# Second feed-forward block: narrower matmuls in its first quarter, and other engines for the weight split in its other three

## The chip, the core and the metric

The kernel runs on one core of a Trainium2 chip. The metric is the device time of one execution in microseconds (us). Two runs of the kernel before took 2849.98 and 2848.92 us, with a median of 2849.45 us.

The engines are named as the profile names them: PE is TensorE's matrix multiplication, PEld its weight loads, DVE is VectorE, ACT is ScalarE, POOL is GpSimd and SP is SyncE, which here issues DMAs. "Columns" of a matmul are the columns of its moving operand; the stationary operand (the "weights" of the array) is 128 x 128 in all matmuls of this text unless said otherwise.

## The reference

One layer of a diffusion trunk over 384 tokens (128 context, 256 latent) of width 2048: a half-step feed-forward block, a mixer (attention and gating), a second half-step feed-forward block, and a final norm.

```python
def swiglu_sublayer(x, g, w_gate, w_up, w_down, shift, scale, gate):
    h = rms_norm(x, g) * (1 + scale) + shift
    f = (jax.nn.silu(h @ w_gate) * (h @ w_up)) @ w_down
    return x + 0.5 * gate * f
...
x_ctx = swiglu_sublayer(x_ctx, ffn2_norm[l], ffn2_w_gate[l], ffn2_w_up[l], ffn2_w_down[l],
                        m_ctx[6], m_ctx[7], m_ctx[8])
...
y_prompt = rms_norm(x_ctx, final_norm)
```

The hidden width is 5632, that is 44 blocks of 128. All tensors are 32-bit floats.

## The kernel before, in words

**The product in three parts.** Activations and weights are each split into an upper part (rounded to the type fp32r) and a lower part (what is left, fp32r too). A product of 128 x 128 weights with one block of activations is three matmuls into the same PSUM bank (`three`): lower weights by upper activations (L256), upper by lower (L257), upper by upper (L258). Each moves 384 columns (386 in a phase's first group, where two extra columns carry the shift). In the built program each matmul has its own weight load; L257 and L258 load the same upper weights one after the other.

**The weight stream.** Weights lie in DRAM as chunks of 128 x 2048 numbers (1 MB). SP loads a chunk into one of three `raw` buffers (`pump`, L205). `ahead` splits one half chunk (128 x 1024) at a time: ACT casts it into a `whi` buffer (L221), then DVE subtracts that from the raw half into a `wlo` buffer (L225). There are four `whi` and four `wlo` buffers. `half`, called by `prod_w` ahead of the matmuls of every half chunk, calls `ahead`, which splits up to the half chunk three places further on; its buffers are those of the half chunk just before the present one. A half chunk feeds 24 matmuls: four banks, two row blocks, three parts.

**The second feed-forward block.** The hidden blocks are cut in quarters of 6, 6, 6 and 4 groups of two hidden blocks (`QUARTERS`). In a quarter each group (`group_gu`; the first of all is `first_group`) takes eight half chunks for its four products (two gate, two up), over all 16 row blocks of the input; `glu` makes silu(gate) * up of them and splits it into `gh` and `gl`. Then `down` multiplies the quarter's hidden blocks by the down weights: four output groups (`dg`) of four banks, each over six half chunks (four in the last quarter). The first three quarters' sums are kept in `x` (`put_y`); the last quarter's are added to x by `add_x`, two DVE instructions for each bank (L578).

**PSUM banks.** Three of a group's four banks come in turn from five `acc` buffers, the fourth from three `mp` buffers.

**Beside it.** Until half chunk 150 after the output projection, modulation tiles are handled: POOL issues a 0.5 MB DMA (`adaw`, L395), DVE multiplies and sums it (L410). That takes in the first two quarters of the second block. In the last quarter `join` reads x back from DRAM (`xo`) and adds it.

**Order.** The program is written out by hand: each engine carries out its instructions in the order of the code, and waits only for the buffers and data it needs.

Of the kernel before, what the change touches and what calls it, by code (L numbers as in the profile page):

```python
# [42 lines left out]
NSEL = 4  # L43
# Half chunks of the weight stream beside which other work is issued: the cached
# keys of each group, the pieces of x kept in DRAM, the splits ahead of the
# groups' ends (LATE), and the modulation tiles (SP0, SP; NREST of them go beside W_out).
KSL = (0, 0, 0, 6)
# [23 lines left out]
def stage_halves(st):  # L71
    """The (group, row block) pairs of each half chunk of a stage."""
    k0, k1 = BLOCKS[st]
    pairs = [(g, k) for g in range(G0) for k in range(k0, k1)]
    return [pairs[i:i + 2] for i in range(0, len(pairs), 2)]


def plan():
    """The order in which the weight chunks are consumed: 'A' chunks go to the
    modulation vectors as they are, 'W' chunks are split for the products."""  # L80
    kinds, pieces = [], []
# [33 lines left out]
class Kernel:  # L115
    def __init__(self, ctx, tc, a):
        self.ctx, self.tc, self.nc, self.a = ctx, tc, tc.nc, a

    # ---------------------------------------------------------------- pools
    def setup(self):  # L120
# [33 lines left out]
        self.late = True  # L154
        self.wide = False
        self.defer = deque()
        self.room = 0
# [6 lines left out]
    def later(self, slot, fn):  # L164
        """Runs fn beside the given half chunk of the stream."""
        self.at.setdefault(max(slot, self.slot), []).append(fn)
# [15 lines left out]

    # -------------------------------------------------------- weight stream
    def pump(self):
        """Loads the next chunks, in the order of use, as far as buffers are free."""
        nc = self.nc
# [22 lines left out]
    def ahead(self, n=NWP, between=None):  # L209
        """Splits the next half chunks, as far as buffers are free; between runs  # L210
        after the first upper part."""
        nc = self.nc
        while len(self.split) < n and self.next_split < len(self.pieces):
            c, half = self.pieces[self.next_split]
            if half is not None:
                if c not in self.raw:
                    break
                src = self.raw[c][:, half * 1024:(half + 1) * 1024]
                hi = self.wp.tile([P, 1024], F32R, tag="whi", name="whi")
                lo = self.wp.tile([P, 1024], F32R, tag="wlo", name="wlo")  # L220
                nc.scalar.copy(hi, src)  # L221
                if between is not None:
                    between()
                    between = None
                nc.vector.tensor_sub(lo, src, hi.bitcast(F32))  # L225
                self.split[self.next_split] = (hi, lo)
                if half == 1:
                    self.done(c)
            self.next_split += 1
# [6 lines left out]
    def half(self):  # L236
        """The next half chunk's two parts; runs what goes beside it."""
        if not self.late or self.pos not in self.split:
# [12 lines left out]

    # ------------------------------------------------------------- products
    def three(self, bank, wh, wl, xh, xl, first, last, n):
        nc = self.nc
        o, xh, xl = bank[:, :n], xh[:, :n], xl[:, :n]
        nc.tensor.matmul(o, lhsT=wl, rhs=xh, start=first, stop=False)  # L256
        nc.tensor.matmul(o, lhsT=wh, rhs=xl, start=False, stop=False)  # L257
        nc.tensor.matmul(o, lhsT=wh, rhs=xh, start=False, stop=last)  # L258

    def prod_w(self, banks, xs, kts, first, last, after=None, n=T):  # L260
        """banks[u] += W[kts, u]^T @ xs[kts] over one half chunk."""
        hi, lo = self.half()
# [8 lines left out]
    def prod_x(self, banks, xs, kts, first, last, after=None):  # L271
        """banks[tt] += xs[kts, tt]^T @ W[kts] over one half chunk."""
        nc = self.nc
# [15 lines left out]

    # ----------------------------------------------------------- modulation  # L290
    def ada_rows(self):
        """silu of both conditioning vectors, padded to 32 stationary columns."""
        nc = self.nc
# [37 lines left out]
    def ada_unit(self, sb, unit, nk):  # L331
        """The rows of sums become columns, added over the four column groups."""
        nc = self.nc
# [24 lines left out]
    def scales(self, j, cg, k0=0, k1=KT):  # L358
        """s = norm gain * (1 + scale) of modulation triple j."""
        nc = self.nc  # L360
# [7 lines left out]
    def csb_load(self, kh, slot):  # L368
        """silu of half of both conditioning vectors, on all partitions."""
        nc = self.nc  # L370
# [46 lines left out]

    # ----------------------------------------------------------------- norm
    def square(self, src):
# [11 lines left out]
    def grown(self, kt, ssq, raw, settle=True):  # L431
        """A new row block of x goes into the norm and, if it may, into the next
        operand; what the vector engine does of it comes one block later."""
        if raw:
# [15 lines left out]
    def rstd(self, sums, width):  # L450
        """1 / sqrt(mean + eps) of each token, on all partitions."""
        nc = self.nc
# [31 lines left out]
    def make_raw(self, *kts):  # L484
        """x scaled, without the token's norm factor and the shift."""
        for kt in kts:
# [24 lines left out]
    def raw_out(self, src, rs):  # L511
        """The products of the raw operand: the tokens' part times their norm
        factor, and the shift's part, to be added to it."""
        nc = self.nc
# [5 lines left out]

    # ------------------------------------------------------------------ ffn
    def glu(self, gi, u, src, rs=None, c=None):
# [25 lines left out]
    def lagged(self):  # L548
        """The lower part of the last g, which need not hold up what comes next."""
        if self.lag is not None:  # L550
# [3 lines left out]
    def first_group(self, ssq, after):  # L554
        """A phase's first group: on the raw operand, while the norm factors and
        the rest of the phase's operand are made. after(u, bank, rs) ends it."""
        banks = [self.bank(u) for u in range(4)]
# [23 lines left out]
    def put_y(self, kt, src, first):  # L581
        """The sum over the quarters' products, where x was."""
        if first:
# [4 lines left out]
    def join(self, ng, src, gate):  # L588
        """Beside the up products of the last quarter: x + gate * y."""
        free = range(2 * ng, 2 * G0)  # L590
# [58 lines left out]
    def first_quarter_staged(self):  # L649
        """The first groups over one block of rows at a time, with the partial  # L650
        sums kept where the groups' products will lie."""
        nc = self.nc
# [63 lines left out]

    # ---------------------------------------------------------------- mixer
    def open_mix(self, st):
# [55 lines left out]

    # attention of one head pair, in pieces
    def att_bias(self, pair, e):
# [103 lines left out]

    # gMLP
    def group_vg(self, j):
# [65 lines left out]
    def out_h(self, rs, *kts):  # L948
        """The mixer's own normalized outputs take h's place."""
        nc = self.nc  # L950
# [55 lines left out]
    def mixer_tail(self, hf):  # L1006
        """The gated half of the mixer's outputs, made beside the other half's products."""
        if hf == 0:
# [28 lines left out]

    # ----------------------------------------------------------------- all
    def spread(self, runs, first, end):
        """The queued modulation tiles, evenly over the half chunks first to end  # L1040
        that end no group; runs: how many of them, and for which half of the
        conditioning vectors (None: the one that is there)."""
        gap = ACTD + 2
# [12 lines left out]
    def run(self):  # L1056
# [90 lines left out]
        with ExitStack() as st:  # L1147
# [8 lines left out]
            for qi, n in enumerate(QUARTERS):  # L1156
                if qi == len(QUARTERS) - 1:
                    self.half_gate(8)
                    self.join(n, self.keep, self.m[8])
                for g in range(n):  # L1160
                    if qi == 0 and g == 0:
                        self.first_group(ssq, lambda u, bank, rs: self.glu(0, u, bank, rs))
                    else:
                        self.group_gu(g)
                lastq = qi == len(QUARTERS) - 1
                if lastq:
                    ssq = self.tmp("ssq")
# [11 lines left out]
def chunks(w, cols):  # L1179
    """[rows, n] -> [128, 2048] blocks of the columns given as slices, each of  # L1180
    as many 128-row parts side by side as fit."""
    import numpy as np
# [122 lines left out]
```

## Time and profile before

| | |
|---|---|
| runs | 2849.98 and 2848.92 us, median 2849.45 us |
| profiled execution | span 2848.6 us, the only time that the page gives of it; 0.85 us under the median of the runs |
| PE busy | 2816.9 us, 99% of the span |
| DVE busy | 1820.1 us, 64% |
| ACT busy | 1018.3 us, 36% |
| POOL busy | 155.5 us, 5% |
| granted TensorE clock | 0.997 |
| DMA | 524.91 MB, mean 184 GB/s |

A row of the groups of instructions reads: line, engine, operation, tile written <- tiles read, shape, count | busy us, mean ns of one | idle time of the engine just before them and what ended it. Matmuls are pipelined, so that the duration in a matmul's row is longer than the distance from one start to the next; that distance is read from the timeline or from a window's length and count. A row of the windows view gives the stretch, the busy time (and count) of PE, PEld, DVE, ACT and POOL, the granted clock, the DMA engines' share and the GB/s.

### The profile page before, as it was taken

To read this page: it belongs to the slowest core of one execution; us is meant where nothing else is said; L and a number is where in the kernel's file an instruction comes from. 1 tells how busy PE (TensorE), PEld (TensorE's weight loads), DVE (VectorE), ACT (ScalarE), POOL (GpSimd) and SP (SyncE) were. 2 spreads that over 40 slices of the span, in tenths; PEclk is the share of its full clock that TensorE was granted. 3 is DMA by queue.
4 is the path that set the end of the run, shared out by engine and by line. 5 is a ranking of instruction groups with operands and counts; after the bars stand their busy time and mean duration, and the time that the engine had idled before them with its cause. 6 is when DMAs were issued, how large, how long until landed. Compare 5 with 4: busy or idle time off the path is not lost.

```text
span 2848.6 us, 39204 instructions
## 1 busy us (share of the span) xinstructions
PE 2816.9 (99%) x16054; PEld 2719.1 (95%) x16054; DVE 1820.1 (64%) x2851; ACT 1018.3 (36%) x1453; POOL 155.5 (5%) x270
## 2 busy tenths in 40 slices
PE   7999999999999999999999999999999999999997
PEld 6889999999999999988888999999999999999997
DVE  4777888789888788764555888444444543333345
ACT  3345433322332234553334535333333223322342
POOL 0000011011111010000000000000000000000000
PEclk9999999999999999999999999999999999999999
DMA  8874566666666675444332663444444433333432
GB/s 335 306 283 173 191 236 231 223 228 247 233 226 240 232 255 200 157 160 145 115 119 104 245 234 128 163 163 148 174 145 164 154 139 120 128 124 127 167 126 85
DMA packets 98308, 524.91 MB, mean 184 GB/s; under 512 B 10832, under 2 KB 18384, under 8 KB 52176
## 3 DMA queue, kind: packets, MB, share of 16 engines
q1 hardware_dynamic: 61648, 371.39, 36.1%
q0 software_dynamic: 36480, 151.01, 15.2%
q8 instruction: 126, 2.06, 0.3%
q14 instruction: 54, 0.44, 0.0%
HBM read 511.88 MB, written 10.49 MB: 183 GB/s over the span
## 4 chain that ended last, share of the span: by engine, by line
PE 52%; DVE 0%; ACT 0%; issue 0%; DVEq 0%
PE acc L256 13%; PE acc L258 12%; PE acc L257 12%; PE mp L256 4%; PE mp L258 4%; PE mp L257 4%; PE acc L281 1%; PE acc L282 1%; PE acc L283 1%; PE mp L796 1%; DVE x L1173 0%; PE mp L870 0%; PE mp L840 0%; PE mp L916 0%; PE mp L456 0%; PE mp L865 0%
## 5 line engine op out<-in xcount | busy, mean ns | idle before, releaser
L225 DVE TENSOR_TENSOR wlo<-raw,whi 128x1024 fp32r<-128x1024 f32 x640 | 783.5, 1226 | 841.1 <-ACT whi L221 840.2
L221 ACT CAST whi<-raw 128x1024 fp32r<-128x1024 f32 x640 | 670.7, 1049 | 1421.4 <-PE mp L258 1148.7
L256 PE MATMUL acc<-hh,wlo 128*128 128x384 f32 (+1 forms) x2760 | 939.7, 340 | 0.0
L258 PE MATMUL acc<-hh,whi 128*128 128x384 f32 (+1 forms) x2760 | 933.0, 338 | 0.0
L257 PE MATMUL acc<-hl,whi 128*128 128x384 f32 (+1 forms) x2760 | 931.0, 337 | 0.0
L256 PEld LDWEIGHTS acc<-hh,wlo 128*128 128x128 f32 x2760 | 519.7, 188 | 31.8 <-issue 16.5
L257 PEld LDWEIGHTS acc<-hl,whi 128*128 128x128 f32 x2760 | 521.0, 189 | 0.8
L258 PEld LDWEIGHTS acc<-hh,whi 128*128 128x128 f32 x2760 | 519.7, 188 | 0.0
L256 PE MATMUL acc<-gh,wlo 128*128 128x384 f32 x1056 | 357.7, 339 | 0.4 <-ACT x L584 0.4
L257 PE MATMUL acc<-gl,whi 128*128 128x384 f32 x1056 | 354.3, 336 | 0.0
L258 PE MATMUL acc<-gh,whi 128*128 128x384 f32 x1056 | 352.8, 334 | 0.0
L410 DVE CUSTOM_DVE_ANT_0 scr<-adaw,csb,m 128x1024 bf16<-128x1024 f32 x208 | 266.8, 1283 | 3.8
L410 DVE CUSTOM_DVE_ANT_0 scr<-adaw,csb,par 128x1024 bf16<-128x1024 f32 x208 | 266.7, 1282 | 3.7
L258 PE MATMUL mp<-hh,whi 128*128 128x384 f32 (+1 forms) x688 | 232.4, 338 | 0.0
L256 PE MATMUL mp<-hh,wlo 128*128 128x384 f32 (+1 forms) x688 | 231.8, 337 | 0.0
L257 PE MATMUL mp<-hl,whi 128*128 128x384 f32 (+1 forms) x688 | 231.6, 337 | 0.0
L256 PEld LDWEIGHTS acc<-gh,wlo 128*128 128x128 f32 x1056 | 198.0, 188 | 0.7 <-ACT x L584 0.7
L258 PEld LDWEIGHTS acc<-gh,whi 128*128 128x128 f32 x1056 | 198.5, 188 | 0.0
L257 PEld LDWEIGHTS acc<-gl,whi 128*128 128x128 f32 x1056 | 198.3, 188 | 0.0
L395 POOL DMA_DIRECT2D adaw<-wada_t x208 | 110.1, 530 | 1457.2 <-DVE m L410 1378.8
L257 PEld LDWEIGHTS mp<-hl,whi 128*128 128x128 f32 x688 | 129.7, 189 | 0.0
L256 PEld LDWEIGHTS mp<-hh,wlo 128*128 128x128 f32 x688 | 129.5, 188 | 0.0
(163 smaller groups left out, 2251.0 us busy)
## 6 DMA issues: line engine op xcount, KB each, us to landing
raw<-ws SPq DMA_DIRECT2D x320, 1024.0 KB, 4.9
adaw<-wada_t POOLq DMA_DIRECT2D x208, 512.0 KB, 4.1
rawa<-wada_s POOLq DMA_DIRECT2D x34, 1024.0 KB, 5.7
csb<-crow POOLq DMA_DIRECT2D x6, 1024.0 KB, 7.6
keep<-x SPq DMA_DIRECT2D x8, 768.0 KB, 7.4
rawa<-wada_s SPq DMA_DIRECT2D x5, 1024.0 KB, 6.6
bias<-bias SPq DMA_DIRECT2D x16, 256.0 KB, 5.1
xo<-xT SPq DMA_DIRECT2D x16, 192.0 KB, 5.8
```

The lines of the kernel that those rows point to most:

```text
L221: nc.scalar.copy(hi, src)
L225: nc.vector.tensor_sub(lo, src, hi.bitcast(F32))
L256: nc.tensor.matmul(o, lhsT=wl, rhs=xh, start=first, stop=False)
L257: nc.tensor.matmul(o, lhsT=wh, rhs=xl, start=False, stop=False)
L258: nc.tensor.matmul(o, lhsT=wh, rhs=xh, start=False, stop=last)
L281: nc.tensor.matmul(o, lhsT=xh, rhs=wl, start=first and kk == 0, stop=False)
L282: nc.tensor.matmul(o, lhsT=xl, rhs=wh, start=False, stop=False)
L283: nc.tensor.matmul(o, lhsT=xh, rhs=wh, start=False, stop=last and kk == 1)
L395: self.nc.gpsimd.dma_start(out=t, in_=self.a["wada_t"][j - 2, kt, kh])
L410: nc.vector.tensor_tensor_reduce(out=scr, in0=t, in1=self.csb[:, v, :], scale=1.0, scalar=init, op0=ALU.mult, op1=ALU.add, accum_out=acc)
L796: nc.tensor.matmul(b[:, :T], lhsT=self.qT[i][rows, pr, TC + P * q:TC + P * (q + 1)], rhs=self.kT[i][rows, pr, TC:CW], start=True, stop=True)
```

## The change

All of it is in the second feed-forward block. In the first quarter, groups 2 to 6 cut each of the three matmuls in two of 192 columns, and the quarter's `down` cuts each in three of 128 columns; the first group stays as it is. In the second quarter every other subtraction is made by GpSimd instead of VectorE. In the third VectorE makes the cast that ScalarE made. In the fourth the upper part comes by a DMA from GpSimd's queue, which reads the same half chunk from DRAM a second time and casts it on the way; the raw chunk is still loaded for the subtraction.

```diff
@@ ahead
-                nc.scalar.copy(hi, src)
+                if self.how == "cast":
+                    w = self.order["W"].index(c)
+                    nc.gpsimd.dma_start(out=hi, in_=self.a["ws"][w][:, half * 1024:(half + 1) * 1024])
+                elif self.how == "vector":
+                    nc.vector.tensor_copy(hi, src)
+                else:
+                    nc.scalar.copy(hi, src)
...
-                nc.vector.tensor_sub(lo, src, hi.bitcast(F32))
+                eng = nc.gpsimd if self.how == "pool" and self.next_split % 2 else nc.vector
+                eng.tensor_sub(lo, src, hi.bitcast(F32))
@@ three
+        if self.cuts > 1:
+            w = n // self.cuts
+            for i in range(self.cuts):
+                c = slice(i * w, (i + 1) * w)
+                nc.tensor.matmul(o[:, c], lhsT=wl, rhs=xh[:, c], start=first and i == 0, stop=False,
+                                 skip_group_check=True)
+                nc.tensor.matmul(o[:, c], lhsT=wh, rhs=xl[:, c], start=False, stop=False, skip_group_check=True)
+                nc.tensor.matmul(o[:, c], lhsT=wh, rhs=xh[:, c], start=False,
+                                 stop=last and i == self.cuts - 1, skip_group_check=True)
+            return
@@ run, second feed-forward block
+                self.how = ("plain", "pool", "vector", "cast")[qi]
                 for g in range(n):
                     if qi == 0 and g == 0:
                         self.first_group(ssq, lambda u, bank, rs: self.glu(0, u, bank, rs))
                     else:
+                        self.cuts = 2 if qi == 0 else 1
                         self.group_gu(g)
                 lastq = qi == len(QUARTERS) - 1
+                self.cuts = 3 if qi == 0 else 1
```

The rest of the diff takes comments out and moves line numbers by up to 22.

On PE, at the end of the first quarter's last group and the start of its `down` (`hh`, `hl`: upper and lower input; `gh0`, `gl0`: upper and lower part of the first hidden block), before:

```order
L256 MATMUL mp_16538<-hh_87,wlo_16663 128x384
L257 MATMUL mp_16538<-hl_88,whi_16662 128x384
L258 MATMUL mp_16538<-hh_87,whi_16662 128x384
L256 MATMUL acc_16795<-gh0_15086,wlo_16699 128x384
L257 MATMUL acc_16795<-gl0_15087,whi_16698 128x384
L258 MATMUL acc_16795<-gh0_15086,whi_16698 128x384
L256 MATMUL acc_16795<-gh1_15088,wlo_16699 128x384
```

The same place in the changed program, with one row of the group and the whole first block of the `down`:

```order
L272 MATMUL mp_17306<-hh_87,whi_17526 128x192
L269 MATMUL acc_17755<-gh0_15086,wlo_17587 128x128
L271 MATMUL acc_17755<-gl0_15087,whi_17586 128x128
L272 MATMUL acc_17755<-gh0_15086,whi_17586 128x128
L269 MATMUL acc_17755<-gh0_15086,wlo_17587 128x128
L271 MATMUL acc_17755<-gl0_15087,whi_17586 128x128
L272 MATMUL acc_17755<-gh0_15086,whi_17586 128x128
L269 MATMUL acc_17755<-gh0_15086,wlo_17587 128x128
L271 MATMUL acc_17755<-gl0_15087,whi_17586 128x128
L272 MATMUL acc_17755<-gh0_15086,whi_17586 128x128
L269 MATMUL acc_17755<-gh1_15088,wlo_17587 128x128
```

Where three matmuls stood for one block, nine stand now, into the same bank, with the lower and the upper weights named anew for each third of the columns. In the whole program PE has 960 matmuls more from the five groups and 1152 more from the `down`.

On POOL, the end of its list before (`csb`: the conditioning vectors, `adaw`: a modulation tile):

```order
L375 DMA csb<-crow 128x2x1024
L395 DMA adaw<-wada_t 128x1024 x18
L375 DMA csb<-crow 128x2x1024
L395 DMA adaw<-wada_t 128x1024 x14
L1294 UNCONDITIONAL_BRANCH
```

And now, from the last four modulation tiles on:

```order
L234 TENSOR_TENSOR wlo<-raw,whi 128x1024 x3
L414 DMA adaw<-wada_t 128x1024
L234 TENSOR_TENSOR wlo<-raw,whi 128x1024
L414 DMA adaw<-wada_t 128x1024
L234 TENSOR_TENSOR wlo<-raw,whi 128x1024 x3
L414 DMA adaw<-wada_t 128x1024
L234 TENSOR_TENSOR wlo<-raw,whi 128x1024 x2
L414 DMA adaw<-wada_t 128x1024
L234 TENSOR_TENSOR wlo<-raw,whi 128x1024 x2
L225 DMA whi<-ws 128x1024 x45
L1316 UNCONDITIONAL_BRANCH
```

POOL now has 36 subtractions among the modulation tiles of the second quarter, and 45 casting DMAs of 0.5 MB behind all of them. The third quarter puts 72 casts on DVE ahead of the subtractions they belong to, and ACT has 117 casts fewer in all.

More of the change, by code (lines that the diff above doesn't have):

```diff
@@ L155, in setup @@
         self.wide = False
+        self.cuts = 1
+        self.how = "plain"
         self.defer = deque()
```

## The prediction, made before the changed kernel ran

> **What bounds the kernel now.** I read the page's head first, for the engine that is never idle.
>
> ```profile
> span 2848.6 us, 39204 instructions
> PE 2816.9 (99%) x16054; PEld 2719.1 (95%) x16054; DVE 1820.1 (64%) x2851; ACT 1018.3 (36%) x1453; POOL 155.5 (5%) x270
> PEclk9999999999999999999999999999999999999999
> ```
>
> PE is busy through the whole span at full clock. Next I asked for windows over the second feed-forward block: groups 2 to 6 of its first quarter, that quarter's `down`, and the three other quarters.
>
> ```profile
> core 0: us, PE busy (x) PEld busy (x) DVE busy (x) ACT busy (x) POOL busy (x), PEclk, DMA share, GB/s
> 1755.90:1924.20 168.30, 168.30 (x961) 168.28 (x960) 94.12 (x139) 61.38 (x84) 4.24 (x8) 1.00 0.42 150
> 1924.20:2024.50 100.30, 100.30 (x577) 100.30 (x577) 45.35 (x50) 32.44 (x40) 3.17 (x6) 1.00 0.44 158
> 2024.50:2327.00 302.50, 302.50 (x1731) 302.47 (x1730) 150.23 (x179) 88.74 (x98) 8.66 (x16) 1.00 0.44 155
> 2327.00:2629.30 302.30, 302.30 (x1729) 302.27 (x1729) 110.81 (x116) 86.55 (x96) 0.00 (x0) 1.00 0.35 126
> 2629.30:2831.00 201.70, 201.70 (x1154) 201.50 (x1152) 87.53 (x121) 74.02 (x109) 0.00 (x0) 1.00 0.34 120
> ```
>
> In none of them does PE wait. It has 5 x 192 = 960 matmuls in the first stretch and 576 in the second: 168.3 / 960 = 0.175 us and 100.3 / 576 = 0.174 us from one 384-column matmul to the next. DVE is busy at most 56% and ACT 37% of any of these stretches. So PE's stream is the time of the block, and anything that stretches a matmul's step counts in full; work that only moves between the other engines counts where it makes PE wait.
>
> **First quarter: more matmuls of fewer columns.** The number of columns moved stays the same. What doubles and triples is the loads: one 128 x 128 load for each matmul. The question is how fast a load can follow a load. The main stream can't show it, since there 0.175 us lie between loads. Two places with narrow matmuls can.
>
> ```profile
> L257 PEld LDWEIGHTS acc<-gl,whi 128*128 128x128 f32 x1056 | 198.3, 188 | 0.0
> L916 PEld LDWEIGHTS mp<-wsT,vg 128*128 128x128 f32 x48 | 6.5, 191 | 0.3
> L338 PEld LDWEIGHTS mp<-par,adasb 128*128 128x128 f32 x40 | 5.4, 191 | 1.0 <-DVE adasb L326 1.0
> ...
> 140.07 0.75 PEld L338 LDWEIGHTS mp<-par,adasb 128*128 128x128 f32 x6
> ...
> 1485.12 0.81 PEld L916 LDWEIGHTS mp<-wsT,vg 128*128 128x128 f32 x6
> 1485.29 0.83 PE L916 MATMUL mp<-wsT,vg 128*128 128x128 f32 x6
> ```
>
> L338 moves only four columns with each 128 x 128 load. Six of its loads stand in one row: 0.75 us from the start of the first to the end of the last, which itself takes 0.191. That leaves (0.75 - 0.191) / 5 = 0.112 us from load to load, with next to nothing for the matmul to do. So the load sets that pace. L916 (128 columns, f32) agrees: the mean of its matmuls is 275 ns in the group's row, so (0.83 - 0.275) / 5 = 0.111.
>
> ```profile
> L916 PE MATMUL mp<-wsT,vg 128*128 128x128 f32 x48 | 6.6, 274 | 0.0
> ```
>
> These are loads of f32 and the stream's are fp32r, but a load's own time is alike, 188 against 191 ns, so I take 0.112 us for fp32r. On columns alone a 192-column matmul would take half of 0.175, 0.088 us, and one of 128 a third, 0.058. Both are under 0.112, so both cases become bound by the load, and cutting to 192 or to 128 costs the same per matmul:
>
> - groups 2 to 6: 1920 x 0.112 = 215.0 us in place of 168.3, **+46.7**;
> - `down`: 1728 x 0.112 = 193.5 us in place of 100.3, **+93.2**.
>
> Nothing hides this: PE is the path. Upward, L916's loads with the first one counted give (0.81 - 0.191) / 5 = 0.124, and the sum would be 69.8 + 114.0 = 183.8; downward 0.111 gives 136.3. A pace below 0.111, or another rate for narrow fp32r matmuls, is left to the rivals. The splits and the bank readers of this quarter get more time than before.
>
> Against this stands a rule: the Trainium skill ("TensorE: Matmul & The Clock Gate", section "Back-to-back issue gap") gives about 81 ns a matmul for a sustained stream of load and matmul at 128 columns. By it the `down` would take, as an estimate, 1728 x 81 ns = 140 us, 40 more and not 93. Its section on LDWEIGHTS gives columns / 1.2 GHz, that is 107 ns for 128 columns, and the row's 112 is near this one; the rows here contradict the 81 for 32-bit loads.
>
> **Second quarter: every other subtraction on GpSimd.** 36 subtractions leave DVE. A half chunk lasts 24 x 0.175 = 4.2 us. Its split begins when PE lets go of the buffers of the half chunk before the present one, and is needed three half chunks later, so it has 12.6 us.
>
> ```profile
> L225 DVE TENSOR_TENSOR wlo<-raw,whi 128x1024 fp32r<-128x1024 f32 x640 | 783.5, 1226 | 841.1 <-ACT whi L221 840.2
> L221 ACT CAST whi<-raw 128x1024 fp32r<-128x1024 f32 x640 | 670.7, 1049 | 1421.4 <-PE mp L258 1148.7
> ...
> L782 POOL TENSOR_TENSOR bias<-bias,par x16: 1275/1292/2332, 1190.8 to 1483.8; 128x512 f32<-128x512 f32 x16
> ```
>
> GpSimd's one two-input operation, on half the elements, took 1.29 us in the middle and 2.33 in the one case that lay across an L225. Twice that is 2.6 to 4.7 us. With ACT's 1.05 a split ends 3.6 to 5.7 us after it may start, and POOL has one such piece in 8.4 us. At least 6.9 of the 12.6 us are left; even held up by a modulation DMA ahead of it in POOL's queue, PE sees nothing. **0**, and no gain, since DVE wasn't waited for. Without that cover each late split would cost PE its lateness, 36 times. Behind a waiting subtraction POOL queues modulation DMAs, which are issued two tiles ahead of their use.
>
> **Third quarter: the cast on DVE.** The nearest one-input rows on DVE:
>
> ```profile
> L809 DVE TENSOR_SCALAR s<-s,mx 128x384 f32<-128x384 f32 x32 | 12.0, 418 | 0.6
> L910 DVE TENSOR_SCALAR vg<-vg,st 128x128 f32<-128x128 f32 x24 | 4.9, 283 | 0.1
> ```
>
> They rise by 135 ns in 256 columns, so 1024 columns would take 0.76 us; the two-input 1.23 is the other end. 72 casts add 55 to 89 us to 110.8 in a window of 302.3. Cast and subtraction end at most 2.5 us after their start, against 2.3 before. DVE's reading of finished banks stands behind both, at most 0.2 us later than before. **0**.
>
> **Fourth quarter: the upper part by casting DMA.** 45 transfers of 0.5 MB, one per 4.2 us, beside the raw stream: twice the window's 120 GB/s. The kernel has a stretch of that kind, the first feed-forward block with its modulation tiles, which are 0.5 MB from POOL's queue too:
>
> ```profile
> raw<-ws SPq DMA_DIRECT2D x66, 1024.0 KB, 6.2
> adaw<-wada_t POOLq DMA_DIRECT2D x107, 512.0 KB, 4.1
> ...
> 500.00:1060.00 560.00, 560.00 (x3203) 559.95 (x3202) 468.85 (x645) 169.69 (x196) 58.01 (x109) 1.00 0.67 235
> ...
> DMA to landing us min/median/max: 3.5/4.1/8.6
> L395 POOL DMA_DIRECT2D adaw<-wada_t x208 | 110.1, 530 | 1457.2 <-DVE m L410 1378.8 <-DVE t L498 76.1 <-issue 2.3
> ```
>
> At 235 GB/s a 0.5 MB transfer lands 4.1 us after its issue, 8.6 at worst there, and PE is never late. Without a price for the cast itself, a split then takes 0.53 + 4.1 + 1.23 = 5.9 us of its 12.6. What comes too late is another thing: the subtraction, now 5.9 us into a half chunk, stands in DVE's queue ahead of `add_x`, which frees the first bank of a finished output group.
>
> ```profile
> L578 DVE SCALAR_TENSOR_TENSOR x<-acc,m,x 128x256 f32<-128x256 f32 x36 | 17.1, 476 | 0.0
> L578 DVE SCALAR_TENSOR_TENSOR x<-acc,m,x 128x128 f32<-128x128 f32 x36 | 12.4, 345 | 9.3 <-PE acc L258 9.3
> ```
>
> That bank is free at 5.9 + 0.82 = 6.7 us. The next group takes two spare `acc` buffers and needs this one for its third bank, half way through its first half chunk, at 4.2 + 2.1 = 6.3 us: 0.4 us late, at three group ends. **+1**; at 8.6 us to landing it is 4.9 each, +15; with an earlier landing nothing.
>
> **The sum.** 46.7 + 93.2 + 1 = 141 us on the profiled span of 2848.6, 2989.6. The median of the runs is 0.85 above that span: **2990 us**. This case's own range is 2975 to 3050, from the bounds 136 and 184 + 15.
>
> **Rivals.**
>
> *Loads that don't bind* (within 2%). If fp32r loads, or loads of the weights that are already there (L257, L258), follow each other faster than f32 loads, the columns set the pace and the total is that of before, 2850. The place is every cut matmul; both parts take (1920 + 1728) p - 268.6 us more, which is 2% (57 us) at a step p of 0.089 us. For it: nothing shows back-to-back fp32r loads. Against it: the equal 188 and 191 ns. The skill's 81 ns belongs here; its estimate would be 2890. Chance 7%.
>
> *Narrow fp32r matmuls run at another rate.* All fp32r matmuls of the trace move 384 columns or more. An f32 product of L916 takes two instructions (48 for 24 products), 0.222 us for 128 columns, 0.333 for 192. At that rate the parts take 1920 x 0.333 = 639 and 1728 x 0.222 = 384 us, +754: 3604. At one such instruction for each matmul (0.111 and 0.167) it is +244: 3094. Against it: nothing in the rows ties a rate to the width. Chances 15% and 5%.
>
> *The cast slows the DMA engines.* Loads of 0.524 MB at the queues' pace
>
> ```profile
> q1 hardware_dynamic: 61648, 371.39, 36.1%
> q0 software_dynamic: 36480, 151.01, 15.2%
> ```
>
> (371.39 MB in 0.361 x 2848.6 us is 361 GB/s, the other 349) take all engines 1.45 + 1.50 = 2.95 of 4.2 us. If a cast took four times as long, a half chunk would need 7.45 us and 45 of them 146 us more: 3136. At under 1.8 times it hides. Chance 7%.
>
> That GpSimd's subtraction needs over 8.4 us, or that something else happens, has 1%.
>
> **How the numbers follow.** The forecast has 65%. A range of 2860 to 3140 holds it, the 3094, nearly all of the DMA case and the upper half of the first rival, about 80%. Within 2% (2793 to 2906), about what a measurement of this kernel can tell from no change, lies only the first rival: 6%, with 1% below and 93% above.
>
> **What would show it.** Between groups 2 and 6 and in the `down` the loads should stand 0.11 us apart for 192 and 128 columns alike, PE without idle time, and the two stretches last 215 and 194 us. 192-column steps of 0.09 would speak for the first rival; steps of 0.22 or more, unequal for the two widths, for the second. The second and third quarter should stay at 302 us. In the fourth `whi` should land about 4 us after its issue, and PE wait at three group ends only. The prediction is wrong if a step is under 0.1 or over 0.13 us, or if the last quarter grows by over 15 us.

## The result and the profile after

The changed kernel took 2991.3 us in the median of two runs (2991.28 and 2991.32) against 2849.45 before: a ratio of 1.0498, 95% interval 1.0467 to 1.0528. The prediction said 2990. Its profiled execution has a span of 2989.1 us.

The windows view of the changed kernel, over groups 2 to 6, the first quarter's `down`, and the other three quarters (columns as before: stretch, then PE, PEld, DVE, ACT and POOL busy with their counts, clock, DMA share, GB/s):

```profile
1755.40:1969.80 214.40, 214.40 (x1922) 214.40 (x1921) 94.87 (x139) 61.89 (x84) 4.24 (x8) 1.00 0.34 119
1969.80:2162.70 192.90, 192.90 (x1730) 192.90 (x1730) 45.41 (x50) 32.41 (x40) 2.64 (x5) 1.00 0.23 80
2162.70:2465.10 302.40, 302.40 (x1730) 302.37 (x1730) 110.65 (x143) 88.80 (x98) 95.80 (x53) 1.00 0.43 157
2465.10:2767.50 302.40, 302.40 (x1730) 302.37 (x1729) 160.69 (x188) 11.64 (x24) 0.00 (x0) 1.00 0.35 126
2767.50:2971.30 203.80, 202.22 (x1154) 201.33 (x1152) 86.94 (x121) 27.60 (x64) 23.84 (x45) 1.00 0.71 235
```

Against the windows of before the five stretches grew by 46.1, 92.6, 0, 0 and 2.1 us, together 140.8; the spans differ by 140.5. In the first two PE and its loads are busy all the time, at full clock: nothing waits, the steps are longer. 1920 matmuls in 214.4 us are 0.1117 us each, and 1728 in 192.9 us 0.1116. The timeline of PE in the two stretches shows the steps one by one:

```profile
1800.30 0.27 PE L269 MATMUL acc<-hh,wlo 128*128 128x192 f32 x1
1800.41 0.27 PE L271 MATMUL acc<-hl,whi 128*128 128x192 f32 x1
1800.52 0.28 PE L272 MATMUL acc<-hh,whi 128*128 128x192 f32 x1
1800.64 0.27 PE L269 MATMUL acc<-hh,wlo 128*128 128x192 f32 x1
...
2000.27 0.28 PE L269 MATMUL mp<-gh,wlo 128*128 128x128 f32 x1
2000.38 0.28 PE L271 MATMUL mp<-gl,whi 128*128 128x128 f32 x1
2000.49 0.27 PE L272 MATMUL mp<-gh,whi 128*128 128x128 f32 x1
2000.60 0.28 PE L269 MATMUL mp<-gh,wlo 128*128 128x128 f32 x1
```

The step is 0.11 us for 192 columns and for 128. L271 and L272 load the same upper weights one after the other, and the second of them comes no sooner.

The groups of instructions show what the other ways to split cost on their engines, and the DMA view of the last quarter the casting transfers:

```profile
L234 POOL TENSOR_TENSOR wlo<-raw,whi 128x1024 fp32r<-128x1024 f32 x36 | 86.9, 2414 | 260.5 <-ACT whi L229 260.5
L227 DVE CAST whi<-raw 128x1024 fp32r<-128x1024 f32 x72 | 49.9, 693 | 129.0 <-PE mp L277 129.0
...
q0 software_dynamic: 6480, 23.60, 37.4%
q1 hardware_dynamic: 5184, 24.12, 33.6%
whi<-ws POOLq DMA_DIRECT2D x45, 512.0 KB, 5.0
```

GpSimd's subtraction takes 2.41 us against 1.23 on DVE. DVE's cast takes 0.69 us against 1.05 on ACT. The casting DMA lands 5.0 us after its issue. In that window of 204 us the casting queue moved 23.60 MB in 0.374 x 204 = 76.3 us of all engines, 309 GB/s, and the raw queue 24.12 MB in 68.5 us, 352 GB/s: for the same bytes a cast took the engines 1.14 times as long. (Before, plain transfers of GpSimd's own queue moved 349 GB/s by the same working.)

The waits view of the changed kernel from the second quarter to the end, asked for PE and then for its loads, is short; what it has beside these rows belongs to the final norm (L475):

```profile
PE acc L275 <- DVE x L597: 1.6, 2, 0.9
...
PEld acc L275 <- issue: 2.5, 3, 1.2
```

Here alone the new splits reach PE: it waits for `add_x` (L597), which frees a bank. The timelines of the three engines show it at the end of the last `down`'s second output group, from the first matmul of the group's last half chunk to the late one of the next group:

```profile
2932.45 0.33 PE L275 MATMUL acc<-gh,wlo 128*128 128x384 f32 x1
2932.91 0.53 POOL L225 DMA_DIRECT2D whi<-ws  x1 [3.66 <-PE mp L277]
2937.74 1.23 DVE L234 TENSOR_TENSOR wlo<-raw,whi 128x1024 fp32r<-128x1024 f32 x1 [3.11 <-DMA whi<-ws]
2939.77 0.41 PE L275 MATMUL acc<-gh,wlo 128*128 128x384 f32 x1 [0.89 <-DVE x L597]
```

### The profile page after: what moved, and what is told of

The parts are those of the page before. It is cut to its first block, busy times and chain, and to the rows that moved or that the text cites. A ratio compares the mean times of both kernels' runs of the same rounds, so it can differ in the third digit from the quotient of the medians.

```text
span 2989.1 us, 43446 instructions
## 1 busy us (share of the span) xinstructions
PE 2957.2 (99%) x18166; PEld 2858.3 (96%) x18166; DVE 1830.6 (61%) x2887; ACT 897.6 (30%) x1336; POOL 265.7 (9%) x351
## 4 chain that ended last, share of the span: by engine, by line
PE 49%; issue 5%; POOL 1%; DVE 1%; ACT 0%; DMA 0%; POOLq 0%; DVEq 0%
PE acc L275 8%; PE acc L277 8%; PE acc L276 8%; PE acc L272 3%; PE acc L269 3%; PE acc L271 3%; PE mp L275 2%; PE mp L277 2%; PE mp L276 2%; PE mp L269 1%; PE mp L272 1%; PE mp L271 1%; PE acc L300 1%; PE acc L301 1%; PE acc L302 1%
## 5 line engine op out<-in xcount | busy, mean ns | idle before, releaser
L229 ACT CAST whi<-raw 128x1024 fp32r<-128x1024 f32 x523 | 548.0, 1049 | 1237.0 <-PE mp L277 729.7
L275 PE MATMUL acc<-hh,wlo 128*128 128x384 f32 (+1 forms) x2520 | 858.9, 341 | 0.0
L277 PE MATMUL acc<-hh,whi 128*128 128x384 f32 (+1 forms) x2520 | 851.9, 338 | 0.0
L276 PE MATMUL acc<-hl,whi 128*128 128x384 f32 (+1 forms) x2520 | 850.1, 337 | 0.0
L275 PEld LDWEIGHTS acc<-hh,wlo 128*128 128x128 f32 x2520 | 474.5, 188 | 31.8 <-issue 16.0
L276 PEld LDWEIGHTS acc<-hl,whi 128*128 128x128 f32 x2520 | 475.7, 189 | 0.8
L275 PE MATMUL acc<-gh,wlo 128*128 128x384 f32 x912 | 309.1, 339 | 2.0 <-DVE x L597 1.6
L276 PE MATMUL acc<-gl,whi 128*128 128x384 f32 x912 | 306.0, 336 | 0.0
L277 PE MATMUL acc<-gh,whi 128*128 128x384 f32 x912 | 304.7, 334 | 0.0
L272 PE MATMUL acc<-hh,whi 128*128 128x192 f32 x480 | 132.1, 275 | 0.0
```

The lines of the kernel that those rows point to most:

```text
L272: nc.tensor.matmul(o[:, c], lhsT=wh, rhs=xh[:, c], start=False, stop=last and i == self.cuts - 1, skip_group_check=True)
```

## The experiments

### The splits without the cuts

```diff
-                        self.cuts = 2 if qi == 0 else 1
+                        self.cuts = 1
...
-                self.cuts = 3 if qi == 0 else 1
+                self.cuts = 1
```

> The cuts are taken out again (384 columns everywhere), the three other ways to split stay. Theory: of the 141.9 us, 139.6 belong to the narrow matmuls and 2.3 to the last quarter's down, where add_x stands behind a subtraction that waits for the casting DMA. So 2851 to 2852 us, second and third quarter 302.4 us each, last quarter 203.8. Rival: the splits cost more or less beside full-width matmuls than beside narrow ones, since PE then takes half chunks faster in the first quarter; then 2850 or under, or over 2855.

Measured: 2852.47 us in the median of ten runs against 2849.72, ratio 1.0009, interval 1.0000 to 1.0019; the span of its profile is 2850.4. Its windows for quarters two to four:

```profile
2024.70:2327.10 302.40, 302.40 (x1730) 302.37 (x1729) 110.64 (x143) 88.84 (x98) 95.89 (x53) 1.00 0.43 157
2327.10:2629.50 302.40, 302.40 (x1729) 302.37 (x1729) 160.67 (x188) 11.65 (x24) 0.00 (x0) 1.00 0.35 126
2629.50:2832.70 203.20, 202.19 (x1153) 201.27 (x1152) 87.05 (x121) 27.62 (x64) 23.87 (x45) 1.00 0.71 236
```

The median lies half a microsecond over the 2851 to 2852 us expected. The second and third quarter are free, and the last costs 1.5 us more than before. So the narrow matmuls are the whole of the change but for two to three microseconds. The two parts don't act on each other: the spans with and without the cuts differ by 138.7 us (2989.1 and 2850.4), and the two narrow stretches grew by 46.1 + 92.6 = 138.7.

### Other widths

```diff
-            w = n // self.cuts
-            for i in range(self.cuts):
-                c = slice(i * w, (i + 1) * w)
+            widths = {2: (256, 128), 3: (96, 96, 96, 96)}[self.cuts]
+            e = 0
+            for i, w in enumerate(widths):
+                c = slice(e, e + w)
+                e += w
...
-                                 stop=last and i == self.cuts - 1, skip_group_check=True)
+                                 stop=last and i == len(widths) - 1, skip_group_check=True)
...
-                self.how = ("plain", "pool", "vector", "cast")[qi]
+                self.how = "plain"
```

> Splits as before the change; groups 2 to 6 cut each matmul in 256 and 128 columns, the down in four of 96. Theory (one load per 0.112 us, columns at 0.4375 ns each plus 7 ns, read from 175 at 384 and 231 at 512): 256 columns step 0.119, 128 and 96 step 0.112. Groups: 960 x (0.119 + 0.112) = 222 us; down: 2304 x 0.112 = 258 us. Rival (the step falls with the width and 192 and 128 were alike by chance): 96 columns well under 0.112, down under 240 us; or 256 columns at twice 0.0875 or more, groups over 270 us.

Measured: 3291.76 us. The windows of the groups, of the first 3.3 us of the `down`, and of a piece from its middle:

```profile
1753.50:1976.00 222.50, 222.50 (x1927) 222.50 (x1926) 95.93 (x142) 62.68 (x86) 4.25 (x8) 1.00 0.33 114
...
1976.20:1979.50 3.30, 3.30 (x32) 3.30 (x31) 1.60 (x2) 1.46 (x2) 0.00 (x0) 1.00 0.00 0
...
2400.00:2420.00 20.00, 20.00 (x96) 20.00 (x95) 3.72 (x5) 1.04 (x1) 0.53 (x1) 0.50 0.08 27
```

The groups took 222.5 us where the theory had 222: 222.5 / 960 = 0.232 us for a pair of 256 and 128 columns, 0.116 a matmul in the mean. Less the 0.112 of 128 columns this would leave 0.120 for 256, but the starts don't show that split: after the first 128-column matmul of three the next came in 0.06 us, after the first 256-column one in 0.16.

```profile
1800.04 0.22 PE L271 MATMUL acc<-hh,wlo 128*128 128x128 f32 x1
1800.10 0.27 PE L273 MATMUL acc<-hl,whi 128*128 128x128 f32 x1
...
1800.33 0.33 PE L271 MATMUL acc<-hh,wlo 128*128 128x256 f32 x1
1800.49 0.28 PE L273 MATMUL acc<-hl,whi 128*128 128x256 f32 x1
```

The `down` missed both theories: 488 us (1976.1 to 2464.6) instead of 258. It began at the expected step, but 3.4 us into it the granted clock fell from 1.00 to 0.50 and stayed there to the end of the stretch, and the step became 0.213 us. No engine waited for another: PE and its loads are busy throughout.

```profile
2099.76 0.41 PE L271 MATMUL acc<-gh,wlo 128*128 128x96 f32 x1
2099.97 0.41 PE L273 MATMUL acc<-gl,whi 128*128 128x96 f32 x1
2100.18 0.41 PE L274 MATMUL acc<-gh,whi 128*128 128x96 f32 x1
2100.39 0.41 PE L271 MATMUL acc<-gh,wlo 128*128 128x96 f32 x1
```

A step of 0.213 us at half clock and of 0.112 at full clock fits a load counted in PE's own clock cycles with about 5 ns added at the full clock (0.213 / 2 = 0.107). The clock came back some 3 us after the next quarter's 384-column matmuls, again with full loads, had begun at 2464.55:

```profile
2465.00 0.52 PE L278 MATMUL acc<-hl,whi 128*128 128x384 f32 x1
2465.32 0.52 PE L279 MATMUL acc<-hh,whi 128*128 128x384 f32 x1
...
2467.56 0.35 PE L277 MATMUL acc<-hh,wlo 128*128 128x384 f32 x1
2467.75 0.34 PE L278 MATMUL acc<-hl,whi 128*128 128x384 f32 x1
```

Why the clock fell was open, and one of the later runs was spent on it.

### Half the load

```diff
+            m = P if first else 64
+            o, wh, wl = bank[:m, :n], wh[:, :m], wl[:, :m]
             for i in range(self.cuts):
...
-                self.how = ("plain", "pool", "vector", "cast")[qi]
+                self.how = "plain"
```

> Splits as before the change; the cuts of 192 and 128 stay, but except for the first row block of each product only 64 of the 128 stationary columns are loaded, so that half of the outputs lack those products. Theory (the load sets the step, by its columns): a load of 64 columns takes half, 0.056, and the columns moved then set the step: 0.088 for 192, 0.060 for 128. Groups 1920 x (0.112 / 16 + 0.088 x 15 / 16) = 172 us, down 1728 x (0.112 / 12 + 0.060 x 11 / 12) = 111 us. Rival (a load and a matmul take 0.112 us to issue, whatever they hold, or narrow fp32r matmuls take 0.112): 214 and 193 us as in the changed kernel.

Measured: 2869.06 us. The windows of groups 2 to 6 and of the `down`:

```profile
1756.50:1931.60 175.10, 175.10 (x1922) 175.10 (x1921) 94.15 (x139) 61.32 (x84) 4.24 (x8) 1.00 0.41 145
1931.60:2043.20 111.60, 111.60 (x1731) 111.60 (x1729) 45.40 (x50) 32.46 (x40) 3.17 (x6) 1.00 0.41 143
```

175 and 112 us, where the theory said 172 and 111 and the rival 214 and 193. Without the first blocks' full loads a 128-column step is (111.6 / 1728 - 0.112 / 12) x 12 / 11 = 0.060 us. The moving operand, the number of instructions and their order are those of the changed kernel; only the stationary columns are halved, and with them the rows of the output, and the extra time is nearly gone. (A time spent on the output would grow with the columns moved; the step with full loads is the same for 192 and for 128.) So it was neither the issue of the instructions nor a slow rate of narrow fp32r matmuls.

### The casting DMA's 2 us

```diff
             for hf in range(2 * nch):
+                self.hold = final and hf == 2 * nch - 1
                 self.prod_w(banks, g_of, (2 * hf, 2 * hf + 1), hf == 0, hf == 2 * nch - 1, after)
+                if self.hold:
+                    self.hold = False
+                    self.ahead()
```

With `hold` set, `half` doesn't call `ahead`.

> The changed kernel, but at the end of each output group of the last quarter's down the next split is issued behind add_x instead of ahead of it. Theory: the 2.3 us by which that down grew (69.05 against 66.75 us) are PE's waits for a bank that add_x frees late, because the subtraction ahead of it on DVE waits for the casting DMA. Then the waits for add_x go, the down takes 66.8 to 67.2 us, the whole 2989.0. Rival (the weights come late, or the double DMA traffic slows PE's loads): 69 us as before, or more, since the split now starts later.

Measured: 2988.92 us. The last quarter's `down` takes 66.75 us again, from the start of its first matmul to that of its last, as before the change, and the waits for `add_x` are gone. The window over the last quarter:

```profile
2766.00:2969.00 203.00, 203.00 (x1162) 202.93 (x1160) 87.77 (x123) 27.62 (x64) 23.84 (x45) 1.00 0.72 236
```

PE is busy in all of it (the window begins 1.5 us early), with the same DMA traffic of 236 GB/s and with splits that start later at the group ends. It was the order on DVE, not the traffic.

### The clock at 96 columns

The `down` in four cuts of 96 columns, with the half loads from above; the groups ahead of it uncut.

```diff
-            w = n // self.cuts
-            for i in range(self.cuts):
+            k = 4 if self.cuts == 3 else 1
+            w = n // k
+            m = P if first else 64
+            o, wh, wl = bank[:m, :n], wh[:, :m], wl[:, :m]
+            for i in range(k):
...
-                self.how = ("plain", "pool", "vector", "cast")[qi]
+                self.how = "plain"
...
-                        self.cuts = 2 if qi == 0 else 1
+                        self.cuts = 1
```

> Splits as before the change, groups uncut; the down of the first quarter cut in four of 96 columns, and except for the first row block of each product only 64 of 128 stationary columns are loaded (half of the outputs lack those products). In the run with 96 columns and full loads the granted clock fell to 0.5 and the step was 0.213 us. Theory: the clock falls because columns move in too small a share of the time (96 columns take about 0.040 of a 0.112 us step, 36%; 128 take 0.053, 48%, and kept the clock). With half loads the step is about 0.058, the share 69%: clock 1.0, down 2304 x (0.112 / 12 + 0.058 x 11 / 12) = 144 us. Rival (the clock falls with matmuls as narrow as 96): clock 0.5, steps 0.107 to 0.213, down 260 us or more.

Measured: 2894.7 us, and for the `down`:

```profile
1924.30:2068.90 144.60, 144.60 (x2306) 144.60 (x2305) 45.42 (x50) 32.48 (x40) 3.17 (x6) 1.00 0.32 111
```

144.6 us at clock 1.00, to the theory's 144. Matmuls of 96 columns as such don't lower the clock. In the `down` the two runs differ in the load, and with it in the share of a step in which columns move. (They differ ahead of it too, where the groups are uncut here.) 384 columns stepped in 0.320 us at half clock, so that a column takes 0.417 ns at full clock, as an estimate: 40 ns for 96 columns and 53 for 128, 36% and 48% of the 0.112 us with full loads. That this share is what the clock follows, with a limit between the two, fits these stretches and the return of the clock with 384 columns, but it isn't shown: no run varied the share alone.

The step itself, without the first blocks, is (144.6 / 2304 - 0.112 / 12) x 12 / 11 = 0.058 us. That is more than 96 columns need, and it is half of 0.107 with the same 5 ns added: here a load of 64 columns sets the step.

### All of the second quarter's subtractions on GpSimd

```diff
-                eng = nc.gpsimd if self.how == "pool" and self.next_split % 2 else nc.vector
+                eng = nc.gpsimd if self.how == "pool" else nc.vector
```

> The changed kernel, with all instead of half of the second quarter's subtractions on GpSimd. Theory (the split has 12.6 us and GpSimd's subtraction, 2.39 us in the changed kernel, needs one per 4.2 us): 72 x 2.39 = 172 of 302 us on POOL, cast and subtraction 3.5 us, PE doesn't wait, second quarter 302.4 us, whole 2991. Rival (GpSimd's queue, with the modulation tiles' DMAs behind subtractions, or DVE held up by GpSimd, is near its limit): PE waits, second quarter over 306 us.

Measured: 2989.87 us. The group row of the subtraction and the window of the quarter:

```profile
L234 POOL TENSOR_TENSOR wlo<-raw,whi 128x1024 fp32r<-128x1024 f32 x72 | 183.0, 2542 | 168.7 <-ACT whi L229 168.5
...
2162.10:2464.50 302.40, 302.40 (x1730) 302.37 (x1729) 98.90 (x99) 88.48 (x98) 191.84 (x89) 1.00 0.45 157
```

POOL is busy for 192 of 302 us and PE doesn't notice. The subtraction took 2.54 us in the mean instead of the 2.39 reckoned with (183 us in all, not 172); one was needed every 4.2 us, so that the margin was still large.

### Fewer buffer pairs

```diff
-NWP = 4
+NWP = 3
```

> The changed kernel with three pairs of whi and wlo buffers instead of four, so that a split has two half chunks, 8.4 us, from the release of its buffers to its use. Theory: the casting DMA's split takes 0.53 + 5.0 + 1.23 = 6.8 us, so that it still hides; the last quarter stays at 204 to 207 us, the second and third at 302.4. Rival (the split by DMA already takes nearly the whole 12.6 us, or the landing time hides a queue): the last quarter grows by over 10 us.

The same with `NWP = 2`:

> The changed kernel with two pairs of whi and wlo buffers: a split has one half chunk, 4.2 us. Theory: the third quarter (0.69 + 1.23 = 1.9 us) stays at 302; the second (1.05 + 2.39 = 3.4 us) stays within 302 to 306; in the last each pair goes round in 4.2 + 6.8 = 11.0 us for two half chunks, 5.5 instead of 4.2 each, so 45 x 1.3 = 59 us more: 255 to 270 us. The first feed-forward block may grow too; that isn't judged here. Rival (the order of the instructions, not the buffers, sets when a split begins): the last quarter as in the changed kernel.

Measured: 3002.59 us with three pairs and 3095.19 with two. The window of the last quarter with three pairs, and those of quarters two, three and four with two:

```profile
2768.70:2983.00 214.30, 205.16 (x1153) 202.46 (x1151) 87.72 (x122) 27.61 (x64) 24.36 (x46) 0.99 0.70 230
```

```profile
2200.90:2508.30 307.40, 304.62 (x1731) 302.13 (x1731) 110.68 (x143) 88.83 (x98) 95.74 (x53) 1.00 0.42 154
2508.30:2810.70 302.40, 302.40 (x1730) 302.37 (x1730) 160.77 (x188) 11.64 (x24) 0.00 (x0) 1.00 0.35 126
2810.70:3075.20 264.50, 217.09 (x1153) 203.45 (x1151) 89.70 (x123) 27.59 (x64) 24.88 (x47) 0.98 0.59 189
```

With two pairs the last quarter grew by 60.7 us (59 expected), the third by nothing, and the second by 5.0 us, 1.4 over the end of what was expected. So the buffers set the lead. The rest of this run's growth, 38 us, lies ahead of the second quarter, which the expectation left open. With three pairs the second and third quarter stayed at 302.4 us, but for the last the expectation missed: 214.3 us and not 204 to 207. That is 10.5 us more than in the changed kernel, just over the 10 us at which the rival had been set. The waits view of PE over that quarter names `add_x` and the subtraction:

```profile
PE acc L275 <- DVE x L597: 4.7, 2, 2.6
PE acc L275 <- DVE wlo L234: 4.4, 5, 1.4
...
DMA to landing us min/median/max: 3.8/4.6/8.1
```

I had set the median landing against a spare of 1.6 us. A landing of 8.1 us is longer than that leaves room for, and the timelines show it making a wait:

```profile
2842.79 0.53 POOL L225 DMA_DIRECT2D whi<-ws  x1 [3.67 <-DVE g L558]
2851.01 1.23 DVE L234 TENSOR_TENSOR wlo<-raw,whi 128x1024 fp32r<-128x1024 f32 x1 [5.00 <-DMA whi<-ws]
2852.29 0.44 PE L275 MATMUL acc<-hh,wlo 128*128 128x384 f32 x1 [1.41 <-DVE wlo L234]
```

This cast needed 8.2 us from its issue to the start of its subtraction. The other three waits of over half a microsecond for a subtraction (0.88, 0.56 and 1.40 us) stand behind casts that needed 7.4, 7.6 and 8.2 us. The two waits for `add_x`, 2.1 and 2.6 us, come at group ends, behind 6.0 and 6.6 us.

## Why the prediction was right, point by point

- **The step of a narrow matmul.** Taken as 0.112 us from loads of f32 weights beside four-column matmuls; measured 0.1117 and 0.1116 for the two widths, so that the pace of the f32 loads does hold for fp32r. The two terms, 46.7 and 93.2 us, measured 46.1 and 92.6. That the load sets the step is what the half-load run showed: 64 columns instead of 128 brought the stretches to 175 and 112 us.
- **A pace of 81 ns.** For a sustained stream of load and matmul at 128 columns the Trainium skill ("TensorE: Matmul & The Clock Gate", section "Back-to-back issue gap") gives about 81 ns; here 1728 such pairs in a row took 111.6 ns each, so that the trace doesn't agree. Its section on LDWEIGHTS gives 107 ns for 128 columns, and the trace's step at full clock is near that; at half clock the step was 213 ns, twice as long.
- **The second and third quarter.** Costed at nothing under the cover of the lead; measured nothing. GpSimd's 2.41 us lie just under the range of 2.6 to 4.7, DVE's cast at 0.69 just under that of 0.76 to 1.23. The lead was the cover: with two buffer pairs the second quarter shows 5 us.
- **The fourth quarter.** The mechanism was right, with its place: `add_x` behind a subtraction that waits for the DMA. The term was mis-sized, +1 where the `down` grew by 2.3 us. PE's starts jump from 2920.89 to 2921.91, from 2938.54 to 2939.77 and from 2956.40 to 2956.75. Against a step of 0.175 us it came 0.85, 1.05 and 0.17 us late, where the prediction had 0.4 each time; the first step after each wait took 0.08 us more, and that makes the 2.3. The prediction had taken the 4.1 us landing of a plain transfer. At these three ends the cast needed 4.6, 4.8 and 4.0 us from its issue to the subtraction (the quarter's median landing of 5.0 would be too much). The sum also holds two errors that nearly cancel, and that is luck. The landing time is counted from the start of the issue, so that the issue's 0.53 us stand in it twice. And the issue began 0.46 us after the half chunk's first matmul (2932.91 against 2932.45), which the sum left out.
- **The total.** The two narrow terms were 1.2 us too high together and the last one 1.1 too low. That the forecast came within 1.3 us of the time is in part this luck; that the narrow matmuls are nearly all of the 141 us is not.
- **The rivals.** Loads that don't bind: refuted by the step itself, for repeated weights too. Narrow fp32r matmuls at another rate, which had 20% in its two forms: refuted by the half loads, with 128 columns in 0.060 us; that was a chance for something the trace didn't show rather than for something it suggested. A cast that holds the DMA engines: 1.14 times, under the 1.8 from which it would have mattered. The range, 2860 to 3140, was wide because of these; the forecast's own, 2975 to 3050, would have held the time.

None of the versions beats the kernel before: those that are faster than the changed kernel only take back what the change added, since PE had no idle time to give.

## What to carry to other kernels

Where every matmul loads new 128-column weights, cut the moving operand no narrower than the load takes: here 192, 128 and (at full clock) 96 columns all stepped in 0.112 us, whatever they moved, and 256 with 128 in 0.116 in the mean. A place in the same trace where the load stands almost alone gives that floor before any run. When work moves to an engine with time to spare, its price is not its duration but what stands behind it in the queue it enters: 2.4 us subtractions on GpSimd cost nothing, and a subtraction that waited for a DMA ahead of a bank's reader cost two microseconds until the two were swapped.

## What the runs showed of the hardware

- With 96 columns and full loads PE's granted clock fell to 0.50 some 3.4 us into the stretch although PE and its loads were never idle in the profile, and all steps became 0.213 us. With the same 96 columns and half loads it stayed at 1.00. It came back 3 us after matmuls of 384 columns with full loads had begun.
- The load's time follows its columns: a step of 0.112 us with 128, and of 0.058 with 64, where 96 columns were moved.
- A DMA that casts f32 to fp32r moved 309 GB/s of all-engine time, against 352 for the plain one beside it, and its 0.5 MB landed 5.0 us after the issue in the median, 3.9 to 7.8.
- DVE's one-input cast of 1024 columns took 0.69 us, less than either end drawn from the rows before.
